# Sums of head outputs made in the out stage, x kept in its place (decoder layer, one core)

## The chip, the cores and the metric

The kernel runs on one core of one Trainium2 chip. A time is the device time of one execution in microseconds (us), and a version is judged by the median of its timed runs. Beside these, one execution was recorded by the hardware profiler. Its span is what the trace covers, and all moments named below count from the span's start. PE is the matmul engine (PEld its weight loads), DVE the vector engine, ACT the scalar engine, POOL the GpSimd engine; SP issues most DMAs, and its rows in the trace are issues, not transfers.

## The reference

One decoder layer on 256 rows of width 2048: attention in two groups of 8 heads, an output projection, and a feed-forward part. What matters here is the path from the head outputs over the projection to the input of the feed-forward part:

```python
h = rmsnorm(x, pre_mix_gain)
proj = jnp.einsum('bsd,de->bse', h, w_in)              # q, k, v of 16 heads, each 128 wide
o_sb = stick_breaking_attention(q_sb, k_sb, v_sb)      # heads 0 to 7
o_dl = dilated_attention(apply_rope(q_dl), apply_rope(k_dl), v_dl)   # heads 8 to 15
mixed = concatenate(head_rmsnorm(o_sb, gain), head_rmsnorm(o_dl, gain))   # 256 x 2048
mix_out = jnp.einsum('bse,ed->bsd', mixed, w_out)      # 2048 x 2048
x = x + rmsnorm(mix_out, post_mix_gain)
h = rmsnorm(x, pre_ffn_gain)
f = conv_geglu_ffn(h, w_up, conv_w, conv_b, w_down)    # w_up is 2048 x 11008
x = x + rmsnorm(f, post_ffn_gain)
```

Everything is float32.

## The kernel before

**Arithmetic.** A float32 product is made from rounded pieces: a weight tile `raw` is cast by ACT to `wh` (`high`, L161), DVE subtracts that from `raw` to give `wl` (`low`, L168), and the activations have such a pair as well. PE adds three matmuls for one product: high by high, low by high, high by low.

**Work and rings.** The weights come in chunks of 1 MB (1536 columns for some), listed in `chunks` in the order in which PE uses them. SP loads a chunk as two tiles of up to 128 x 1024 into a ring of five rooms (`raw`, `RAW_BUFS`); `ahead(i)` issues loads two chunks ahead and splits one chunk ahead. `wh` and `wl` have four rooms each. So a load waits until the tile five before it is split, and a cast waits until PE has read a tile some four before it. Beside this, DMAs from SP and POOL (`down.presum`, one step for most chunks) form sums of weight blocks in DRAM: `t13` and `t24` of the out projection (`t_out` in the profile) and of the last matrix (`t_kept`). The order on each engine is set by a scheduler from the order of the code; where `pin` is used, as in the seam between out projection and feed-forward part, the order of the code is kept.

**The attention stage** goes over the 16 heads with `v` and `qk` chunks. Each head is a generator that is advanced after chunks (`step`). The last lines of `stick_head` make the normalised output `y` of one of the heads 0 to 7, split it into `mix[0]` and `mix[1]`, and, after each odd head, form sums for the pair.

**The out stage** multiplies `mix` (rows are heads, 128 each) by `w_out` in four blocks of 512 columns, `c` = 0 to 3, and four blocks of 512 rows, `kq` = 0 to 3. Column blocks 0 and 1, and the lower half of the rows for column blocks 2 and 3 (heads 8 to 15), are plain: 24 matmuls for one `out(c, kq)`. For heads 0 to 7 and column blocks 2 and 3 the kernel uses seven block products in place of eight: a pair of heads (`m` = 0 to 3), two row tiles of `x` and two column blocks form a 2 x 2 by 2 x 2 block product, whose factors are single blocks (chunk `pa`) or sums of blocks (chunk `ts` or `pb`, loaded from `t_out`). The sums of head outputs that multiply them are in the tile `so`: four sums for each pair, in two pieces. The seven results gather in seven accumulators `o`, called `seven` in the code.

**Early sums.** The weight sums of the pairs m = 0 and 1 (`ts`) are loaded and split early, into two tiles `early`, which lie in the two rooms `hT0` and `hT1` of the transposed activations (free between attention and feed-forward part). Those of m = 2 and 3 (`pb`) go through the ordinary ring.

**x.** The tile `x1` holds x for the first norm. Its room is then given to `so`. At `out(3, 2)` a new `x1` is made in that room, and x is loaded a second time (L1122, two DMAs of 1 MB) for the residual.

**The seam.** For each row tile t, after its last out product: squares of `o` (`squares`, L628, ACT), their mean and the root (`mean`, `newton`, L638 to L653), `update` (L1156, DVE: x + r * mix_out), `turn` (L1164, PE transposes into `pth`), `highs` (L1170, ACT) and `lows` (L1176, DVE) that fill `hT` for the first products of the feed-forward part (`mmu`). In the pinned order ACT has three casts of feed-forward weights, and one square of x, between the end of tile 0 and the squares of tile 1:

```python
hs = [high(raw, "up") for raw in raws[i + 1]]
up0.append(low(raws[i + 1][0], hs[0], "up"))
hs.append(high(raws[i + 2][0], "up"))
square(0, 0)
```

The tile `mg` (2 x 2048 columns) takes the projected rows; its columns 1024 to 2047 are written only late in the out stage. The tile `sums` shares one room (tag `on`) with the normalised outputs of heads 8 to 15, which PE transposes.

Of the kernel before, what the change touches and what calls it, by code (L numbers as in the profile page):

```python
# [9 lines left out]
F32 = mybir.dt.float32  # L10
F32R = mybir.dt.float32r
# [5 lines left out]
P = 128  # L17
D = 2048
S = 256
# [16 lines left out]
NPAIR = 17  # L36
LATE_PAIRS = 2
HELD = 4
OUT_PAIRS, SPLIT_EARLY = 4, 2
SINGLE_BEHIND = (0, 2, 4, 5, 7, 9, 11, 12, 14)  # L40


# [59 lines left out]
def layer_kernel(ctx: ExitStack, tc: tile.TileContext, a, out: bass.AP):  # L102
    nc = tc.nc
    V, A, T, G = nc.vector, nc.scalar, nc.tensor, nc.gpsimd

    cpool = ctx.enter_context(tc.tile_pool(name="cpool", bufs=1))
# [14 lines left out]
    HALF = 1024  # L121
# [19 lines left out]
    early = []  # L141

    def split_early(raws, m):
        if not early:
            early.extend(cpool.tile([P, SPLIT_EARLY, 2, HALF], F32R, tag=f"hT{i}", name=f"early{i}") for i in range(2))
        both = []
        for raw, room in zip(raws, early):
            wh, wl = (room[:, m, i, :] for i in range(2))
            A.copy(wh, raw)
            V.tensor_tensor(wl, raw, wh.bitcast(F32), op=ALU.subtract)  # L150
            both.append((wh, wl))
        return both
# [109 lines left out]
    out_cols = lambda c, kq: chunks.append(("out", c, kq, a["w_o"][c, kq], 2048))  # L262
    out_sums = lambda kind, m: chunks.append((kind, m, 0, [k[m] for k in kept_out], 2048))
    out_raw = lambda m: chunks.append(("pa", m, 0, a["w_op"][:, 1536 * m:1536 * (m + 1)], 1536))
    out_cols(0, 0)
    out_cols(0, 1)
    out_sums("ts", 0)
    out_cols(0, 2)
    out_cols(1, 0)
    out_sums("ts", 1)  # L270
    for c, kq in ((1, 1), (1, 2), (0, 3), (1, 3)):
        out_cols(c, kq)
    for m in range(3):
        out_raw(m)
    out_cols(2, 2)
    out_sums("pb", 2)
    out_raw(3)
    out_sums("pb", 3)
# [5 lines left out]
    raws, parts_of, between = {}, {}, {}  # L284
# [24 lines left out]
    hT = [Halves(hT2.tiles, i) for i in range(2)]  # L309

    phA = tc.tile_pool(name="phA", bufs=2)
    apool = phA.__enter__()
    cst = apool.tile([P, C_END - P], F32, name="cst", bufs=1)
    gpre = small.tile([P, KT], F32, name="gpre", bufs=1, padded_shape=[P, KT + 32])
    x1 = apool.tile([P, 2, D], F32, tag="x1", name="x1", bufs=1)
    x1_kept = nc.dram_tensor("x1_kept", (S, D), F32, kind="Internal").ap()

    mix = [apool.tile([P, NH, S], F32R, name=f"mix{i}", bufs=1) for i in range(2)]
    mg = apool.tile([P, 2, D], F32, name="mg", bufs=1)
# [134 lines left out]


    vts = {}
    even, so = [None], []

    banks = []

# [22 lines left out]
    def stick_head(h, qk):  # L483
# [47 lines left out]
        q = apool.tile([P, S], F32, tag="sq", name="q", bufs=1)  # L531
# [2 lines left out]
        V.scalar_tensor_tensor(q, q, 3.0, r0, op0=ALU.subtract, op1=ALU.mult)  # L534
        if h == 0:
            V.tensor_scalar(gain[:, 0:NH], par[:, P_HEAD:P_HEAD + NH], -0.5, None, op0=ALU.mult)
        y = q if h % 2 else apool.tile([P, S], F32, tag="jks", name="even", bufs=1)
        V.scalar_tensor_tensor(y, po, gain[:, h:h + 1], q, op0=ALU.mult, op1=ALU.mult)
        A.copy(mix[0][:, h, :], y)
        V.tensor_tensor(mix[1][:, h, :], y, mix[0][:, h, :].bitcast(F32), op=ALU.subtract)  # L540
        if h % 2 == 0:
            even[0] = y
            return
        m = h // 2
        if m == 0:
            so.append(apool.tile([P, OUT_PAIRS, 2, 4, P], F32R, tag="x1", name="so", bufs=1))
        sums = apool.tile([P, 4, P], F32, tag="on", name="sums", bufs=1)
        a11, a21, a12, a22 = even[0][:, 0:P], even[0][:, P:S], y[:, 0:P], y[:, P:S]
        V.tensor_tensor(sums[:, 0, :], a11, a21, op=ALU.subtract)
        V.tensor_tensor(sums[:, 1, :], a22, a21, op=ALU.subtract)  # L550
        V.scalar_tensor_tensor(sums[:, 2, :], sums[:, 1, :], -1.0, a11, op0=ALU.mult, op1=ALU.subtract)
# [463 lines left out]
    for i, (kind, p, s, _, w) in enumerate(chunks):  # L1015
        parts = ahead(i, 0 if (kind, p, s) == ("out", 3, 3) else SPLITS)
        if kind == "v":
            if s == 0:
                pool, tag = (ps_at, "at") if p == 1 else (ps_mm, "mm")
# [35 lines left out]
        elif kind == "qk":  # L1055
# [7 lines left out]
            if s == 1:  # L1063
                active.append(stick_head(p, qk) if p < 8 else dilated_head(p, qk))
                next(active[-1])
# [46 lines left out]
        elif kind == "out":  # L1112
# [4 lines left out]
                    rows = Rows(mg, "o")  # L1117
            if p == 3 and s == 2:
                held = parts
                x1 = apool.tile([P, 2, D], F32, tag="x1", name="x1", bufs=1)  # L1120
                for t in range(2):
                    nc.sync.dma_start(x1[:, t, :], a["x"][t * P:(t + 1) * P, :])  # L1122
                continue
            if p < 3:
                mm_moving(mm["out", p], parts, mix[0], mix[1], 4 * s, s == 0, s == 3, **(dict(skip_group_check=True) if p == 2 else {}))
                if s == 3:
# [11 lines left out]
            else:  # L1138
# [41 lines left out]
                hT = [Halves(hT2.tiles, i) for i in range(2)]  # L1180
                loose = dict(skip_group_check=True)
                wh, wl = (w[:, 0:512] for w in held[0])
# [200 lines left out]
```

## Time and profile before

| | us |
|---|---|
| median of three timed runs | 1091.31 |
| the three runs | 1088.06 to 1104.67 |
| the profiled execution, device time | 1087.02 |
| its span | 1085.2 |
| PE busy | 1069.1 (99%) |
| DVE busy | 852.7 (79%) |
| ACT busy | 683.8 (63%) |
| POOL busy | 108.9 (10%) |

The profiled execution is 1.8 us longer than its span, and 4.3 us under the median of the timed runs. PE counts as busy from the start of a matmul to its modelled end, so a busy PE may still be waiting briefly between matmuls; idle time of the other engines costs nothing as long as PE has work. The attention stage ends at about 304 us, the out stage lasts to 386, the seam to about 400, and the feed-forward part takes the rest. Rows of the trace are read as: start, duration, engine, line, operation, written tile <- read tiles, count, and in square brackets how long the engine was idle before it and what ended that.

### The profile page before, as it was taken

The numbers are of one execution on the slowest core, as the hardware profiler recorded it, in microseconds if no ns is written. First come the engines' busy times: TensorE is split into PE (matmuls) and PEld (weight loads), VectorE is DVE, ScalarE is ACT, GpSimd is POOL, SyncE is SP. The second block draws the span as 40 slices with busy tenths as digits, with TensorE's granted clock in tenths as the row PEclk, the third lists the DMA queues.
The fourth block names the chain that finished last, engine by engine and source line by source line (L and its number), as shares of the span: only waits on it lengthen the run. The fifth ranks groups of instructions, "written<-read, shape, count | busy, mean of one in ns | idle before, by whom it ended". The sixth has DMA issues, their size and how long they took to land.

```text
span 1085.2 us, 19025 instructions
## 1 busy us (share of the span) xinstructions
PE 1069.1 (99%) x7157; PEld 977.0 (90%) x7157; DVE 852.7 (79%) x1303; ACT 683.8 (63%) x1004; POOL 108.9 (10%) x143
## 2 busy tenths in 40 slices
PE   9999999999999989999999999999999999999996
PEld 7888888888888879999999999999999988888885
DVE  7577876876875778887877878787778699998997
ACT  6667767756764576565655555555555587666775
POOL 0011001111111001121111111111110100000002
PEclk9999999999999999999999999999999999999999
DMA  9998778899898879999999988999999899779993
GB/s 347 360 296 262 211 233 254 235 272 256 243 327 253 279 260 288 333 324 314 330 299 284 276 269 272 275 269 281 276 285 264 266 349 382 269 262 353 394 361 118
DMA packets 101596, 311.52 MB, mean 287 GB/s; under 512 B 10944, under 2 KB 11712, under 8 KB 96320
## 3 DMA queue, kind: packets, MB, share of 16 engines
q1 hardware_dynamic: 94832, 275.68, 71.4%
q0 software_dynamic: 6240, 34.09, 17.7%
q8 instruction: 56, 0.92, 0.3%
q10 hardware_dynamic: 432, 0.53, 0.1%
q14 instruction: 36, 0.29, 0.1%
HBM read 306.07 MB, written 72.35 MB: 349 GB/s over the span
## 4 chain that ended last, share of the span: by engine, by line
PE 92%; DVE 3%; DMA 2%; ACT 2%; issue 1%; DVEq 0%; ACTq 0%
PE mmu L193 42%; PE mmqk L183 9%; PE p L878 6%; PE p L877 6%; PE p L876 6%; PE mmqk L181 5%; PE mmv L230 3%; PE mmv L231 3%; PE mmv L234 3%; DMA raw<-in_w_up 1%; PE mmo L234 1%; PE mmo L230 1%; PE mmo L231 1%; PE mmu L204 1%; DMA raw<-in_w_o 1%; DVE wl L168 1%
## 5 line engine op out<-in xcount | busy, mean ns | idle before, releaser
L168 DVE TENSOR_TENSOR wl<-raw,wh 128x1024 fp32r<-128x1024 f32 x383 | 454.5, 1194 | 161.2 <-ACT wh L161 129.9
L161 ACT CAST wh<-raw 128x1024 fp32r<-128x1024 f32 x383 | 391.8, 1029 | 178.2 <-PE mmu L193 62.9
L193 PE MATMUL mmu<-hT,wh 128*128 128x256 f32 x2688 | 311.9, 276 | 0.0
L193 PEld LDWEIGHTS mmu<-hT,wh 128*128 128x128 f32 x2688 | 308.1, 188 | 0.0
L193 PE MATMUL mmu<-hT,wl 128*128 128x256 f32 x1344 | 159.6, 276 | 0.0
L193 PEld LDWEIGHTS mmu<-hT,wl 128*128 128x128 f32 x1344 | 155.7, 188 | 0.0
L183 PE MATMUL mmqk<-hT,wh 128*128 128x512 f32 x512 | 122.0, 390 | 0.0
L183 PEld LDWEIGHTS mmqk<-hT,wh 128*128 128x128 f32 x512 | 94.8, 188 | 18.9
L692 ACT ACTIVATE cv<-pair,par 128x256 f32<-128x256 f32 x86 | 51.5, 599 | 80.9 <-DVE pair L690 80.5
L786 POOL DMA_DIRECT2D t_kept<-in_w x68 | 53.3, 885 | 351.4 <-DMA t_kept<-in_w_dn 340.3
L876 PE MATMUL p<-wh,yp 128*128 128x512 f32 x210 | 81.7, 389 | 0.0
L877 PE MATMUL p<-wh,yp 128*128 128x512 f32 x210 | 81.7, 389 | 0.0
L878 PE MATMUL p<-wl,yp 128*128 128x512 f32 x210 | 81.7, 390 | 0.0
L181 PE MATMUL mmqk<-hT,wl 128*128 128x256 f32 x512 | 67.9, 279 | 0.0
L181 PEld LDWEIGHTS mmqk<-hT,wl 128*128 128x128 f32 x512 | 63.5, 188 | 1.3
L786 POOL DMA_DIRECT2D t_kept<-t_kept x46 | 35.6, 774 | 266.3 <-DMA t_kept<-t_kept 135.2
L693 DVE SCALAR_TENSOR_TENSOR cv<-pair,par,cv 128x255 f32<-128x255 f32 x86 | 41.2, 480 | 14.8 <-ACT cv L692 14.8
L230 PE MATMUL mmv<-wh,hT 128*128 128x512 f32 x128 | 49.8, 391 | 0.0
L231 PE MATMUL mmv<-wh,hT 128*128 128x512 f32 x128 | 49.7, 390 | 0.0
L878 PEld LDWEIGHTS p<-wl,yp 128*128 128x128 f32 x210 | 39.4, 188 | 8.4 <-DVE wl L168 0.4
L877 PEld LDWEIGHTS p<-wh,yp 128*128 128x128 f32 x210 | 39.4, 188 | 8.3
L876 PEld LDWEIGHTS p<-wh,yp 128*128 128x128 f32 x210 | 39.4, 188 | 8.2
(301 smaller groups left out, 1349.7 us busy)
## 6 DMA issues: line engine op xcount, KB each, us to landing
raw<-in_w_up SPq DMA_DIRECT2D x172, 512.0 KB, 6.4
raw<-in_w_qk SPq DMA_DIRECT2D x64, 512.0 KB, 6.1
t_kept<-in_w_dn SPq DMA_DIRECT2D x57, 512.0 KB, 7.0
t_kept<-in_w POOLq DMA_DIRECT2D x68, 256.0 KB, 6.7
raw<-in_w_dn SPq DMA_DIRECT2D x31, 512.0 KB, 6.3
raw<-t_kept SPq DMA_DIRECT2D x29, 512.0 KB, 6.2
raw<-in_w_v SPq DMA_DIRECT2D x28, 512.0 KB, 5.6
raw<-in_w_o SPq DMA_DIRECT2D x24, 512.0 KB, 5.9
```

The source lines that it names most:

```text
L161: pin(A.copy(wh, raw))
L168: pin(V.tensor_tensor(wl, raw, wh.bitcast(F32), op=ALU.subtract))
L181: T.matmul(ps[:, 0, :], w, h[:, k, 0, :], **edge)
L183: T.matmul(ps, w, h[:, k, :, :], **edge)
L193: pin(T.matmul(ps, w, h[:, k, part, :], start=(i == 0), stop=(i == 3 * KT - 1)))
L230: T.matmul(ps[t], hi[:, k, tc_], ws, start=(first and i == 0 and j == 0), stop=False, **kw)
L231: T.matmul(ps[t], lo[:, k, tc_], ws, start=False, stop=False, **kw)
L692: A.activation(cv, u, AF.Identity, scale=cw(2), bias=par[:, P_CB + f:P_CB + f + 1])
L786: tc.keep_in_program_order(G.dma_start(flat(to), flat(block), accum_op=ALU.add, max_dma_last_dim=8192))
L876: T.matmul(ps, yh, wh[:, cs], start=key not in self.begun, stop=False)
L877: T.matmul(ps, yl, wh[:, cs], start=False, stop=False)
L878: T.matmul(ps, yh, wl[:, cs], start=False, stop=self.left[key] == 0)
```

## The change

1. The normalised output `y` of each of the heads 0 to 7 is written to `mg`, columns 1024 to 2047 (`whole(h)`), not to a passing tile. The sums of a pair are no longer made at the end of each odd head: the code moves to `head_sums(m)`, called in the out stage at the chunks `out(1,0)`, `out(1,1)`, `out(1,2)` and `out(0,3)`.
2. `so` lies in the room `hT0`, and `x1` keeps its room. The second load of x goes.
3. Since `hT0` is taken, only one pair (m = 0) is split early, into one tile in `hT1`. The weight sums of m = 1 become a `pb` chunk, and the chunks of the out stage stand in another order.

The diff, without the parts that only rename:

```diff
-OUT_PAIRS, SPLIT_EARLY = 4, 2
+OUT_PAIRS, SPLIT_EARLY = 4, 1
...
-            early.extend(cpool.tile([P, SPLIT_EARLY, 2, HALF], F32R, tag=f"hT{i}", name=f"early{i}") for i in range(2))
+            early.append(cpool.tile([P, 2, 2, HALF], F32R, tag="hT1", name="early"))
...
-        for raw, room in zip(raws, early):
-            wh, wl = (room[:, m, i, :] for i in range(2))
+        for n, raw in enumerate(raws):
+            wh, wl = (early[0][:, n, i, :] for i in range(2))
...
-    out_cols(0, 0)
-    out_cols(0, 1)
+    for c, kq in ((0, 0), (0, 1), (0, 2), (1, 0)):
+        out_cols(c, kq)
     out_sums("ts", 0)
-    out_cols(0, 2)
-    out_cols(1, 0)
-    out_sums("ts", 1)
     for c, kq in ((1, 1), (1, 2), (0, 3), (1, 3)):
         out_cols(c, kq)
-    for m in range(3):
-        out_raw(m)
+    out_raw(0)
+    out_raw(1)
+    out_sums("pb", 1)
     out_cols(2, 2)
+    out_raw(2)
     out_sums("pb", 2)
...
-        y = q if h % 2 else apool.tile([P, S], F32, tag="jks", name="even", bufs=1)
+        y = whole(h) if h < 2 * OUT_PAIRS else q
...
-        if h % 2 == 0:
-            even[0] = y
-            return
-        m = h // 2
+
+    def whole(h):
+        return mg[:, h // 4, 1024 + h % 4 * S:1024 + (h % 4 + 1) * S]
+
+    def head_sums(m):
         if m == 0:
-            so.append(apool.tile([P, OUT_PAIRS, 2, 4, P], F32R, tag="x1", name="so", bufs=1))
+            so.append(cpool.tile([P, OUT_PAIRS, 2, 4, P], F32R, tag="hT0", name="so"))
         sums = apool.tile([P, 4, P], F32, tag="on", name="sums", bufs=1)
-        a11, a21, a12, a22 = even[0][:, 0:P], even[0][:, P:S], y[:, 0:P], y[:, P:S]
+        a11, a21, a12, a22 = (whole(2 * m + k)[:, t * P:(t + 1) * P] for k in range(2) for t in range(2))
         V.tensor_tensor(sums[:, 0, :], a11, a21, op=ALU.subtract)
         V.tensor_tensor(sums[:, 1, :], a22, a21, op=ALU.subtract)
         V.scalar_tensor_tensor(sums[:, 2, :], sums[:, 1, :], -1.0, a11, op0=ALU.mult, op1=ALU.subtract)
...
             if p == 3 and s == 2:
                 held = parts
-                x1 = apool.tile([P, 2, D], F32, tag="x1", name="x1", bufs=1)
-                for t in range(2):
-                    nc.sync.dma_start(x1[:, t, :], a["x"][t * P:(t + 1) * P, :])
                 continue
+            if (p, s) in ((1, 0), (1, 1), (1, 2), (0, 3)):
+                head_sums(len(done))
+                done.append(p)
```

What this does to the order on the engines, at three places. First SP's queue from the last chunks of the out stage into the seam (`x_3899` is the second tile for x, `x_81` the first). Before:

```order
L129 DMA raw<-in_w_o 128x1024 x6
L782 DMA t_kept<-in_w_dn 128x2x512
L129 DMA raw<-in_w_up 128x1024 x2
L1122 DMA x_3899<-in_x 128x2048 x2
L129 DMA raw<-in_w_up 128x1024 x3
L1149 DMA x_kept<-x_3899 128x2048
L129 DMA raw<-in_w_up 128x1024
```

And now:

```order
L129 DMA raw<-in_w_o 128x1024 x6
L782 DMA t_kept<-in_w_dn 128x2x512
L129 DMA raw<-in_w_up 128x1024 x5
L1149 DMA x_kept<-x_81 128x2048
L129 DMA raw<-in_w_up 128x1024
```

The two loads of x between the second and the third load of feed-forward weights are gone; nothing else moved there.

Second, SP's queue where the seven products run (`in_w_op` is a `pa` chunk, `t_out` a chunk of weight sums). Before:

```order
L129 DMA raw<-in_w_op 128x1024
L129 DMA raw<-in_w_op 128x512
L129 DMA raw<-in_w_o 128x1024 x2
L137 DMA raw<-t_out 128x2x512 x2
L129 DMA raw<-in_w_op 128x1024
L129 DMA raw<-in_w_op 128x512
L137 DMA raw<-t_out 128x2x512 x2
```

And now:

```order
L137 DMA raw<-t_out 128x2x512 x2
L129 DMA raw<-in_w_o 128x1024 x2
L129 DMA raw<-in_w_op 128x1024
L129 DMA raw<-in_w_op 128x512
L137 DMA raw<-t_out 128x2x512 x2
L129 DMA raw<-in_w_op 128x1024
L129 DMA raw<-in_w_op 128x512
L137 DMA raw<-t_out 128x2x512 x2
```

Three loads of weight sums stand here where there were two, and the third `pa` chunk has gone behind `out(2,2)`.

Third, DVE in the out stage, at the last of the heads (`head_674`) and the splits of the following chunks. Before:

```order
L605 TENSOR_SCALAR on<-head_674,rr 128x128 x2
L168 TENSOR_TENSOR wl<-raw,wh 128x1024 x2
L613 SCALAR_TENSOR_TENSOR mix_83<-head_674,par,mix_82 128x256
L168 TENSOR_TENSOR wl<-raw,wh 128x1024 x5
L632 SCALAR_TENSOR_TENSOR mg<-mmo,gbc 128x512
```

And now:

```order
L605 TENSOR_SCALAR on<-head_674,rr 128x128 x2
L168 TENSOR_TENSOR wl<-raw,wh 128x1024
L549 TENSOR_TENSOR sums<-mg 128x128
L550 TENSOR_TENSOR sums<-mg 128x128
L168 TENSOR_TENSOR wl<-raw,wh 128x1024
L551 SCALAR_TENSOR_TENSOR sums<-sums,mg 128x128
L613 SCALAR_TENSOR_TENSOR mix_83<-head_674,par,mix_82 128x256
L552 TENSOR_TENSOR sums<-mg,sums 128x128
L168 TENSOR_TENSOR wl<-raw,wh 128x1024
L554 TENSOR_TENSOR so<-sums,so 128x512
```

The five instructions of a pair's sums stand between the splits of weight tiles, one pair for each chunk; the rows of the other three pairs follow in the same way.

More of the change, by code (lines that the diff above doesn't have):

```diff
@@ L314, in layer_kernel @@
     gpre = small.tile([P, KT], F32, name="gpre", bufs=1, padded_shape=[P, KT + 32])
-    x1 = apool.tile([P, 2, D], F32, tag="x1", name="x1", bufs=1)
+    x1 = apool.tile([P, 2, D], F32, name="x1", bufs=1)
     x1_kept = nc.dram_tensor("x1_kept", (S, D), F32, kind="Internal").ap()
@@ L456, in layer_kernel @@
     vts = {}
-    even, so = [None], []
+    so, done = [], []
     banks = []
@@ L1119, in layer_kernel @@
                 held = parts
-                x1 = apool.tile([P, 2, D], F32, tag="x1", name="x1", bufs=1)
-                for t in range(2):
-                    nc.sync.dma_start(x1[:, t, :], a["x"][t * P:(t + 1) * P, :])
                 continue
+            if (p, s) in ((1, 0), (1, 1), (1, 2), (0, 3)):
+                head_sums(len(done))
+                done.append(p)
             if p < 3:
```

## The prediction

> **What bounds the kernel now.** I read the busy times by stage first, then what PE waited for, then the chain of waits where the two meet. The stages, with PE, PEld, DVE, ACT and POOL busy, the granted clock, the DMA share and GB/s:
> ```profile
> 300.00:344.00 44.00, 43.85 (x210) 35.96 (x209) 29.67 (x55) 25.05 (x53) 6.31 (x8) 1.00 0.95 298
> 344.00:369.00 25.00, 25.00 (x112) 20.68 (x111) 15.41 (x16) 14.04 (x17) 0.00 (x0) 1.00 0.75 236
> 369.00:386.00 17.00, 17.00 (x82) 14.23 (x81) 15.28 (x24) 7.41 (x13) 1.56 (x2) 1.00 0.99 353
> 386.00:400.00 14.00, 8.88 (x62) 7.94 (x60) 10.44 (x24) 10.28 (x27) 0.00 (x0) 0.88 0.72 274
> 400.00:700.00 300.00, 300.00 (x2644) 299.92 (x2644) 237.71 (x376) 173.01 (x228) 44.40 (x57) 1.00 0.94 295
> 700.00:1060.00 360.00, 360.00 (x2316) 326.17 (x2315) 306.24 (x389) 232.94 (x274) 19.35 (x25) 1.00 0.92 306
> ```
> PE has work without a break in the out stage (300 to 386) and again from 400 to 1060. What is won or lost before 400 therefore moves everything behind it by the same amount. Only the seam, 386 to 400, has PE idle (5.1 of 14 us), and there the clock is below full. The waits of PE:
> ```profile
> PE pth L1164 <- DVE x L1156: 4.9, 1, 4.9
> ...
> PE score L567 <- DVE qk L562: 0.7, 2, 0.4
> ```
> The long one is the transposes of the second row tile, which wait for the residual `x`. The chain of waits there (start, us, what):
> ```profile
> 372.20 14.88 DMA raw<-in_w_up
> ...
> 388.86 0.70 ACT jks L628 x2
> ...
> 390.70 0.50 DVE x L1156
> ...
> 391.25 0.70 PE pth L1164 x2
> ```
> So the cause is a weight load that took 14.9 us. The timeline of SP, ACT, DVE and PE shows how it reaches PE:
> ```profile
> 370.85 0.99 SPq L1122 DMA_DIRECT2D x<-in_x  x2
> 372.20 0.33 SPq L129 DMA_DIRECT2D raw<-in_w_up  x1
> ...
> 381.63 1.98 ACT L161 CAST wh<-raw 128x1024 fp32r<-128x1024 f32 x2
> 387.16 1.04 ACT L161 CAST wh<-raw 128x1024 fp32r<-128x1024 f32 x1 [3.54 <-DMA raw<-in_w_up]
> ...
> 384.87 1.22 DVE L168 TENSOR_TENSOR wl<-raw,wh 128x1024 fp32r<-128x1024 f32 x1
> 389.58 0.16 DVE L638 TENSOR_SCALAR_CACHE_REDUCE rj<-sso 128x4 f32<-128x4 f32 x1 [3.49 <-ACT jks L628]
> ...
> 384.42 0.62 PE L234 MATMUL o<-wl,mix 128*128 128x512 f32 x2
> 384.87 1.47 PE L1164 MATMUL pth<-ident,x 128*128 128x128 f32 x12
> 391.25 1.12 PE L1164 MATMUL pth<-ident,x 128*128 128x128 f32 x4 [4.90 <-DVE x L1156]
> ```
> SP issues two loads of `x` just ahead of that weight load. ACT then reaches the cast of the weight early and stands 3.54 us in it. The squares of the second row tile (`jks`) are queued behind the cast, the norm (`rj`) behind the squares, the update of `x` behind the norm, PE behind the update.
>
> **The change, part by part.**
>
> *The two loads of x go.* How long loads take from issue to landing (KB each, us), around the seam:
> ```profile
> raw<-in_w_up SPq DMA_DIRECT2D x1, 512.0 KB, 7.6
> ...
> x<-in_x SPq DMA_DIRECT2D x2, 1024.0 KB, 12.9
> ```
> The one weight load issued just before x took 7.6 us, so the late one would land at 372.2 + 7.6 = 379.8. By the other way, 2.1 MB fewer at the stage's 353 GB/s are 5.9 us, and 387.1 - 5.9 = 381.2. ACT wants it at 381.63 + 1.98 = 383.6, so on either count the wait is gone with 2.4 us or more to spare. What is late next: everything on ACT moves 3.55 us up, and the squares of the second tile, at 388.86 before, would start at 385.31. Their input is ready when PE ends its last `o` product, 384.42 + 0.62 = 385.04, so PE's own work is only 0.27 us from being the limit. DVE would reach `rj` at 389.58 - 3.55 = 386.03, but is busy until 384.87 + 1.22 = 386.09. So 0.06 us is lost and the term is **-3.5 us**; PE's gap shrinks from 4.9 to 1.4 us. Bounds: 0, if the load is as late without x, and -3.5.
>
> *The clock.* The page's row of granted clock over 40 slices, the slices around PE's restart, and ACT's waits for transposes there:
> ```profile
> PEclk9999999999999999999999999999999999999999
> ...
> 390.00:391.00 1.00, 0.00 (x0) 0.00 (x0) 0.93 (x4) 0.81 (x3) 0.00 (x0) 1.00 0.94 389
> 391.00:392.00 1.00, 0.76 (x4) 0.61 (x4) 1.00 (x3) 0.03 (x1) 0.00 (x0) 0.57 0.38 156
> ...
> 393.97 1.57 ACT L1170 ACTIVATE hT<-pth,par 128x256 fp32r<-128x256 f32 x4 [0.43 <-PE pth L1164]
> ...
> 397.90 0.84 ACT L1170 ACTIVATE hT<-pth,par 128x256 fp32r<-128x256 f32 x2 [0.68 <-PE pth L1164]
> ```
> The seam's mean of 0.88 over 14 us is 14 x 0.12 / 0.5 = 3.4 us at half clock, beginning with PE's restart. Had PE alone set the pace, that cost 1.7 us. But ACT feeds PE there, and ACT itself waited for PE's slow transposes only 0.43 + 0.68 = 1.1 us. A gap of 4.9 us brought the clock down, gaps of 0.4 us (the `score` row, in the attention stage) did not, since every slice of the page reads 9 there. A gap of 1.4 us lies nearer to the second, so I take the clock to hold and the term to be **-1.1 us**, with bounds 0 and -1.7. [...]
>
> *The sums of head outputs move from the attention stage to the out stage.* One pair of heads costs (min/median/max ns):
> ```profile
> L549 DVE TENSOR_TENSOR sums<-even x4: 281/281/282, 117.4 to 218.9; 128x128 f32<-128x128 f32 x4
> ...
> L552 DVE TENSOR_TENSOR sums<-q,sums x4: 292/292/295, 119.9 to 221.2; 128x128 f32<-128x128 f32 x4
> L554 DVE TENSOR_TENSOR so<-sums,so x4: 686/692/693, 120.9 to 223.3; 128x512 fp32r<-128x512 f32 x4
> ...
> L553 ACT CAST so<-sums x4: 605/620/624, 120.2 to 222.0; 128x512 fp32r<-128x512 f32 x4
> ```
> That is 4 x 0.29 + 0.69 = 1.85 us of DVE and 0.62 us of ACT, four times: 7.4 and 2.5 us. Where they leave, PE waited for DVE only 0.7 us in all, so they give 0 (bounds 0 and -0.7). Where they arrive (in the stretch from 300 to 344), DVE was busy 29.7 of 44 us and has 37 after, and ACT 27.5. The cover is the ring of split weights: a tile is split three tiles before PE reads it, 3 x 2.7 us. Without that cover each sum would cost its 1.85 us. The first sum waits on DVE for PE's transposes of the last head (its room was theirs); the split of the next tile is queued behind it, with the same cover. **0 us.** Storing the heads' outputs in `mg` instead of `even` is the same instruction to another place: 0.
>
> *One pair's weight sums are no longer split early.* PE's count of products stays; the order of loads changes, and that has a cost only if loads come late. The pace of PE; then the loads in us from issue to landing (the first two rows for 340 to 369, the next row and the spread of the `t_out` loads for 284 to 312); then the split's two halves:
> ```profile
> 344.46 0.23 PE o L1084
> ...
> 355.34 0.23 PE o L1084
> ...
> raw<-in_w_o SPq DMA_DIRECT2D x8, 512.0 KB, 5.6
> raw<-t_out SPq DMA_DIRECT2D x4, 512.0 KB, 4.1
> ...
> raw<-t_out SPq DMA_DIRECT2D x4, 512.0 KB, 6.2
> ...
> DMA to landing us min/median/max: 4.6/6.2/7.0
> ...
> L168 DVE TENSOR_TENSOR wl<-raw,wh 128x1024 fp32r<-128x1024 f32 x10 | 12.1, 1224 | 6.7 <-ACT wh L161 6.6
> L161 ACT CAST wh<-raw 128x1024 fp32r<-128x1024 f32 x11 | 11.4, 1054 | 6.7 <-PE o L1084 4.4 <-PE o L231 1.2 <-DVE wl L168 0.7
> ```
> Sixteen products take 355.34 - 344.46 = 10.88 us, 0.68 each; the first starts at 344.2. In the new order `pa0` with the early sums ends at 349.0, `pa1` and `pb1` at 353.8, `out(2,2)` (8 x 0.68) at 359.2, `pa2` at 361.2, and `pb2`, `pa3`, `pb3` at 368.7 as before. A load goes out when the tile five before it is split. `pb1`'s second tile gets the room of `pa0`'s first (349.0) and is split by 349.0 + 1.05 + 1.22 = 351.3. Then `pb2`'s first tile is loaded, for a time L, and split at 353.6 + L; `pb3`'s second, five tiles on, at 355.9 + 2L. PE wants it at 368.7 - 1.36 = 367.3, so L may be 5.7 us. The weight sums took 4.1 us in this stretch, and the one pair added (1 MB) meets a DMA share of 0.75 there: I take L = 4.1 and **0 us**. At the longest `t_out` load of the out stage, 7.0 us, PE would lose 2 x (7.0 - 5.7) = 2.6 us. Bounds 0 and +2.6.
>
> **The sum.** -3.5 - 1.1 + 0 + 0 = -4.6 us. The profiled execution took 1087.0 us (span 1085.2 and 1.8 around it), so 1082.4 in its terms. The three timed runs have their median at 1091.3, 4.3 above it; against that median the forecast is 1086.7.
>
> **The rivals.**
> - *The clock falls all the same*: the 1.4 us gap is enough, and only -3.5 is left, 1087.8. For it: the seam after the gap is full of short waits for ACT. Against: the 0.4 us gaps.
> - *The load is late without x*: the DMA share was 0.99 from 369 to 386, and if other queues fill the room, the cast waits on. The gain is then 0 to 2 us, 1089 to 1091.3. Against: 7.6 us for the neighbour.
> - *The out stage runs dry, slower than before*: the place is `pb2` to `pb3`, the price 2 x (L - 5.7), and it decides when this exceeds 4.6, at L = 8.0. At L = 9 the time is 1091.3 - 4.6 + 6.6 = 1093.3. For it: 7.0 has been seen at the stage's start, with a higher DMA share. Against: 4.1 in the very stretch, and the two x loads that would compete later are gone.
>
> **How the numbers follow.** Forecast 0.65, clock falls 0.12, load late 0.10, out stage dry 0.08, anything else 0.05. The low end takes all best bounds, -3.5 - 1.7 - 0.7 = -5.9, from the profiled execution: 1081. The high end is the dry out stage: 1093. That leaves out less than 2 in 10. Two per cent, 22 us, is about what a measurement of this kernel can tell from no change, and no case comes near it: faster 0.01, same 0.97, slower 0.02.
>
> **What would show it.** Right: no wait of ACT's cast for `in_w_up` at the seam, PE's longest wait near 1.4 us, clock 1.00 throughout, and a start of the dense stretch some 4.6 us earlier. Wrong: the cast still waits for DMA; PE waits for `wh` or `wl` in 344 to 369; landings of `t_out` above 5.7 us. A new wait of PE anywhere before 344 would break the claim that the moved sums are covered.

## The result and the profile after

The changed kernel took 1082.57 us (median of 6 runs) against 1091.31 in the three runs shown ahead; run beside each other, the ratio of after to before is 0.9933, 95% interval 0.9908 to 0.9959. That is faster by 0.4 to 0.9%, inside the 2% that counts as no change, and 4 us below the forecast of 1086.7, though inside its range of 1081 to 1093. The first ratio rests on only two executions of the kernel before, 1088.06 and 1091.31. Two later sets of runs of the same two kernels gave 0.9960 (0.9944 to 0.9976) and 0.9952 (0.9932 to 0.9972). Some executions of a kernel are 17 us longer, with 281 ns for a product of the up stage instead of 276; the ratios, and the counts and medians below, leave them out, but the profiles of the changed kernel and of E1, E4, E6, E8, E10 and E11 are of such executions, so they are read only up to 410 us, and their last stretch is 0.41 us too long.

Four starts on PE divide the way there: the first product of the value projection at 148 us and of the next one at 222, the first of the seven products, the first transpose `pth`, and `r2ps` in the dense stretch. The timeline of PE in the kernel before (start, us, what):

```profile
148.45 0.39 PE L230 MATMUL mmv<-wh,hT 128*128 128x512 f32 x1
...
222.69 0.39 PE L230 MATMUL mmv<-wh,hT 128*128 128x512 f32 x1
...
344.07 0.39 PE L1083 MATMUL o<-wh,mix 128*128 128x512 f32 x1
...
401.32 1.07 PE L204 MATMUL mmu<-hT,wl 128*128 128x256 f32 x8
...
411.52 0.60 PE L660 MATMUL r2ps<-pair,negones 128*128 128x128 f32 x4
```

And in the changed kernel, with the two groups of transposes:

```profile
148.49 0.39 PE L230 MATMUL mmv<-wh,hT 128*128 128x512 f32 x1
...
221.48 0.39 PE L230 MATMUL mmv<-wh,hT 128*128 128x512 f32 x1
...
342.93 0.39 PE L1083 MATMUL o<-wh,mix 128*128 128x512 f32 x1
...
385.12 1.47 PE L1164 MATMUL pth<-ident,x 128*128 128x128 f32 x12
387.88 0.83 PE L1164 MATMUL pth<-ident,x 128*128 128x128 f32 x4 [1.29 <-DVE x L1156]
...
396.69 1.11 PE L204 MATMUL mmu<-hT,wl 128*128 128x256 f32 x8
...
407.30 0.61 PE L660 MATMUL r2ps<-pair,negones 128*128 128x128 f32 x4
```

With the `pth` rows of before, 384.87 and 391.25, the stretches between these starts are:

| stretch on PE (us) | before | changed | difference |
|---|---|---|---|
| 148 to 222, attention | 74.24 | 72.99 | -1.25 |
| 222 to the seven products | 121.38 | 121.45 | +0.07 |
| seven products to first `pth` | 40.80 | 42.19 | +1.39 |
| first `pth` to second | 6.38 | 2.76 | -3.62 |
| second `pth` to `r2ps` | 20.27 | 19.42 | -0.85 |
| sum | | | -4.26 |

The last stretch of the changed kernel can't be taken as it stands. From the row of eight products (L204) to `r2ps` the same products take 411.52 - 401.32 = 10.20 us before and 407.30 - 396.69 = 10.61 in the changed kernel. At the pace of before, the last difference is -1.26 and the sum -4.67. E12, whose profile has the pace of before, confirms it: second `pth` at 386.48, `r2ps` at 405.50, which is 19.02 us and 1.25 under before.

The seam did what was forecast, two other stretches moved by more than an us each, and these two nearly cancel. The stages of the changed kernel, with the columns of before (PE, PEld, DVE, ACT, POOL, clock, DMA share, GB/s):

```profile
300.00:344.00 44.00, 43.39 (x208) 35.97 (x207) 33.83 (x72) 27.54 (x58) 6.31 (x8) 1.00 0.90 270
344.00:369.00 25.00, 25.00 (x112) 20.67 (x111) 15.42 (x16) 14.07 (x15) 0.00 (x0) 1.00 0.79 265
369.00:386.00 17.00, 16.24 (x75) 12.88 (x74) 16.38 (x25) 10.70 (x19) 1.56 (x2) 1.00 0.86 273
386.00:400.00 14.00, 12.46 (x103) 11.59 (x102) 13.88 (x32) 12.04 (x33) 0.00 (x0) 1.00 0.76 264
```

The clock of the seam is 1.00 where it was 0.88, and PE is busy there 12.46 us where it was 8.88. But PE now has idle time in the two stages that had almost none. The waits of PE from 60 to 400 us (us in total, times, longest):

```profile
PE pth L1164 <- DVE x L1156: 1.3, 1, 1.3
PE head L609 <- DVE on L605: 0.6, 1, 0.6
PE o L230 <- DVE o L1110: 0.6, 1, 0.6
PE o L234 <- DVE wl L168: 0.2, 1, 0.2
PE mmu L204 <- ACT hT L1170: 0.2, 1, 0.2
```

The 4.9 us are 1.3, the two waits for scores (`L567`, 0.7) are gone, and three waits of the out stage and a short one in the seam are new.

*The seam.* ACT and DVE there (timeline):

```profile
381.85 2.93 ACT L161 CAST wh<-raw 128x1024 fp32r<-128x1024 f32 x3
...
385.43 0.60 ACT L628 ACTIVATE jks<-o 128x512 bf16<-128x512 f32 x1
...
386.22 0.15 DVE L638 TENSOR_SCALAR_CACHE_REDUCE rj<-sso 128x4 f32<-128x4 f32 x1
```

Three casts run through with no wait between them; before, the third stood 3.54 us. `rj` comes at 386.22, when DVE ends a split that began at 385.09, as the working had it.

*The loss of 1.39 us.* SP and ACT in the kernel before, from the loads of out(2,3) on:

```profile
358.40 9.46 SPq L129 DMA_DIRECT2D raw<-in_w_o  x6
...
366.39 1.06 ACT L161 CAST wh<-raw 128x1024 fp32r<-128x1024 f32 x1
```

SP, ACT and PE in the changed kernel:

```profile
359.98 6.74 SPq L129 DMA_DIRECT2D raw<-in_w_o  x6
...
359.22 1.57 ACT L161 CAST wh<-raw 128x1024 fp32r<-128x1024 f32 x2 [0.53 <-PE o L1084]
...
367.83 1.05 ACT L161 CAST wh<-raw 128x1024 fp32r<-128x1024 f32 x1 [2.72 <-DMA raw<-in_w_o]
...
374.27 0.50 PE L230 MATMUL o<-wh,mix 128*128 128x512 f32 x1 [0.58 <-DVE o L1110]
```

The casts at 366.39 and 367.83 are of the second tile of out(2,3), counted by the order and the widths of the casts. The first of the six `w_o` loads goes out at 359.98, 1.6 us later than the 358.40 of before, while PE was 1.1 us ahead. The second goes out at 361.56 (360.43 before), behind the split of the cast at 359.22, and takes 6.2 us; ACT waits 2.72 us for it. DVE's row sums (L1108 to L1132) stand behind that tile's split, and PE waits for them. By its starts PE loses 0.74 us at 374.27, where the view shows 0.58, and most of the other 0.65 around the wait for `wl` that the view shows as 0.2.

*The gain of 1.25 us.* It falls at two places, 203 and 216 us. ACT, DVE and PE of the kernel before at the first:

```profile
197.28 2.00 ACT L161 CAST wh<-raw 128x1024 fp32r<-128x1024 f32 x2
199.31 0.62 ACT L558 COPY rot<-qk 64x512 f32<-64x512 f32 x1
...
202.94 0.68 DVE L562 TENSOR_TENSOR qk<-qk,rot 128x512 f32<-128x512 f32 x1
...
202.54 0.84 PE L181 MATMUL mmqk<-hT,wl 128*128 128x256 f32 x5
203.68 0.49 PE L567 MATMUL score<-qk 128*128 128x128 f32 x2 [0.30 <-DVE qk L562]
```

And of the changed kernel:

```profile
196.53 1.05 ACT L161 CAST wh<-raw 128x1024 fp32r<-128x1024 f32 x1
197.60 0.62 ACT L558 COPY rot<-qk 64x512 f32<-64x512 f32 x1
...
200.22 0.69 DVE L562 TENSOR_TENSOR qk<-qk,rot 128x512 f32<-128x512 f32 x1
...
202.66 0.39 PE L567 MATMUL score<-qk 128*128 128x128 f32 x2
202.80 0.36 PE L480 MATMUL score<-qh 128*128 128x256 f32 x1
```

Before, the rotation copies stand on ACT behind two casts from 197.28 on, in the changed kernel behind one; on DVE a split of 1.2 us stands ahead of the last step of the rotation (L562) before, and behind it in the changed kernel. So the copies came 1.7 us later and the next head's finished rows 2.7, and PE had to wait for them behind five products of other work. In the changed kernel PE doesn't wait. No sum runs on DVE between 196 and 204 us in either trace; what differs in this stretch is the order of ACT's and DVE's queues. But in the kernel before a pair's sums end on DVE only at 195.83, and ACT begins the cast ahead of these rows at 195.78, in the changed kernel at 194.54. At the second place the copies come 2.1 us later before (212.36 against 210.27), and no sum runs there from 196 to 218.

### The profile page after: what moved, and what is told of

Read it like the earlier page. It is cut to its first block, busy times and chain, and to the rows that moved or that the text cites. A ratio compares the mean times of both kernels' runs of the same rounds, so it can differ in the third digit from the quotient of the medians.

```text
span 1098.0 us, 19018 instructions
## 1 busy us (share of the span) xinstructions
PE 1085.4 (99%) x7157; PEld 993.3 (90%) x7157; DVE 853.5 (78%) x1303; ACT 684.5 (62%) x1004; POOL 108.9 (10%) x143
## 4 chain that ended last, share of the span: by engine, by line
PE 95%; DVE 2%; DMA 1%; ACT 1%; issue 1%; DVEq 0%; ACTq 0%
PE mmu L193 43%; PE mmqk L183 11%; PE p L876 6%; PE p L878 6%; PE p L877 6%; PE mmqk L181 5%; PE mmv L230 3%; PE mmv L231 3%; PE mmv L234 3%; PE mmo L231 1%; PE mmo L234 1%; PE mmo L230 1%; PE mmu L204 1%; DVE wl L168 1%; DMA raw<-in_w_o 1%
## 5 line engine op out<-in xcount | busy, mean ns | idle before, releaser
L168 DVE TENSOR_TENSOR wl<-raw,wh 128x1024 fp32r<-128x1024 f32 (+1 forms) x385 | 456.7, 1194 | 176.4 <-ACT wh L161 139.9
L161 ACT CAST wh<-raw 128x1024 fp32r<-128x1024 f32 (+1 forms) x385 | 393.7, 1028 | 189.6 <-PE mmu L193 83.3
L193 PE MATMUL mmu<-hT,wh 128*128 128x256 f32 x2688 | 323.7, 281 | 0.0
L193 PEld LDWEIGHTS mmu<-hT,wh 128*128 128x128 f32 x2688 | 319.6, 189 | 0.0
L193 PE MATMUL mmu<-hT,wl 128*128 128x256 f32 x1344 | 165.5, 281 | 0.0
L193 PEld LDWEIGHTS mmu<-hT,wl 128*128 128x128 f32 x1344 | 161.6, 189 | 0.0
```

The lines of the kernel that those rows point to most:

```text
L161: pin(A.copy(wh, raw))
L168: pin(V.tensor_tensor(wl, raw, wh.bitcast(F32), op=ALU.subtract))
L193: pin(T.matmul(ps, w, h[:, k, part, :], start=(i == 0), stop=(i == 3 * KT - 1)))
```

## The experiments

Each kernel was run with a profile and in five rounds beside the kernel before. The stretches by the same starts, in us, and the ratio to before; the starts from which they are subtracted are PE's rows as above:

| kernel | 148 to 222 | to the seven | to `pth` | to `r2ps` | ratio (95%) |
|---|---|---|---|---|---|
| before | 74.24 | 121.38 | 40.80 | 26.65 | 1 |
| changed | 72.99 | 121.45 | 42.19 | 22.18 | 0.9933 (0.9908 to 0.9959) |
| E1 changed, again | 72.99 | 122.30 | 42.64 | 22.20 | 0.9960 (0.9944 to 0.9976) |
| E8 changed, third time | 72.99 | 121.33 | 42.16 | 22.24 | 0.9952 (0.9932 to 0.9972) |
| E2 sums moved only | 72.99 | 121.24 | 40.81 | 27.28 | 0.9989 (0.9978 to 0.9999) |
| E3 changed, x loaded | 73.00 | 121.40 | 42.18 | 27.13 | 1.0000 (0.9992 to 1.0009) |
| E4 before, cast later | 74.29 | 121.76 | 40.80 | 24.79 | 0.9956 (0.9942 to 0.9969) |
| E5 changed, pa2 ahead | 73.00 | 121.36 | 40.80 | 23.40 | 0.9939 (0.9920 to 0.9959) |
| E6 changed, early sums back | 73.00 | 120.87 | 42.41 | 22.16 | 0.9936 (0.9916 to 0.9955) |
| E7 both, seam edited | 73.00 | 120.87 | 40.81 | 22.54 | 0.9938 (0.9920 to 0.9956) |
| E11 the same, again | 72.99 | 120.87 | 41.90 | 22.91 | 0.9931 (0.9906 to 0.9956) |
| E12 both, seam as changed | 72.99 | 120.87 | 40.81 | 21.81 | 0.9938 (0.9925 to 0.9952) |
| E9 before, gap filled | 74.27 | 121.70 | 40.80 | 26.37 | 0.9986 (0.9977 to 0.9996) |
| E10 E7 with gap filled | 73.00 | 120.87 | 41.90 | 22.92 | 0.9940 (0.9920 to 0.9960) |

In the last stretch the changed kernel, E1, E4, E6, E8, E10 and E11 hold the 0.41 us named above. The first stretch repeats far better than the times do: 148 to 222 is 74.24 to 74.29 in three kernels whose attention is as before, and 72.99 or 73.00 in eleven with the sums moved.

**E1, the changed kernel again.**

> The changed kernel once more, to get the size of the change from more executions. My reading of its trace against the trace before, by moments of the same instruction: the first out product of the seven comes 1.2 us earlier (342.9 for 344.1), the first transposes of the seam 0.25 later, the second ones 3.4 earlier, the first feed-forward products after the seam (r2ps) 4.2 earlier. So I expect 4.2 to 4.6 us under the kernel before, a ratio of 0.996. The rival: the 0.9933 of the first measurement (7.3 us) is the true size, and some 3 us come from a place that one pair of traces doesn't show.

The ratio is the 0.9960 expected, and 0.9933 lies outside its interval: the rival found no support. In the profile the wait at head 14 (L609) is 1.4 us instead of 0.6, and the one for L1110 is 1.0 instead of 0.6: these waits vary.

**E2, only the sums moved.** The kernel before with the sums made in the out stage; they stay in the room of `x1`, so x is loaded again, two pairs are split early and the loads keep their order:

```
-        y = q if h % 2 else apool.tile([P, S], F32, tag="jks", name="even", bufs=1)
+        y = whole(h) if h < 2 * OUT_PAIRS else q
...
+            if (p, s) in ((1, 0), (1, 1), (1, 2), (0, 3)):
+                head_sums(len(done))
+                done.append(p)
```

> The kernel before with one part of the change: the outputs of heads 0 to 7 kept in mg and the sums of pairs made in the out stage; so stays in the room of x, x is loaded a second time, two pairs of weight sums are split early, and the chunks stand in the old order. Theory: the 1.2 us won before the seven products come from DVE and ACT work taken out of the attention stage; then the first of the seven products stands near 342.9 here too, the gap of PE at the seam stays 4.9 us with the clock falling, and the kernel is about 1 us faster than before (ratio 0.999). Rival: they come from the new order of loads; then the first product stays at 344.1 and the ratio is 1.000.

PE and ACT of this kernel:

```profile
221.41 0.39 PE L230 MATMUL mmv<-wh,hT 128*128 128x512 f32 x1
```

```profile
196.47 1.05 ACT L161 CAST wh<-raw 128x1024 fp32r<-128x1024 f32 x1
197.54 0.62 ACT L559 COPY rot<-qk 64x512 f32<-64x512 f32 x1
```

The attention stage gives the whole 1.25 us, with ACT in the order of the changed kernel, and the out stage loses nothing (121.24 and 40.81). So the gain in attention belongs to the moved sums, and the loss in the out stage does not. Whether it comes from DVE's time for the sums or from the order that the scheduler chose without them isn't separated. The time fell only 0.1%: the seam took 27.28, 0.6 more than before, with the clock at half for 6.8 us instead of 3.4.

**E3, the changed kernel with x loaded after all.** Two loads of 1 MB at the old place, into a room that nothing reads:

```
+                again = cpool.tile([P, 2, D], F32, tag="hT0", name="again")
+                for t in range(2):
+                    nc.sync.dma_start(again[:, t, :], a["x"][t * P:(t + 1) * P, :])
```

> The changed kernel with the two 1 MB loads of x put back at their old place in SP's queue, into the room hT0, which is empty then; nothing reads them. Theory: the loads alone make the third feed-forward weight load late (about 15 us for 5.8), ACT waits 3 to 4 us in the cast, PE's gap is again near 4.9 us and the clock falls to half for 3.4 us; the kernel loses 4 to 4.5 us and comes out level with the kernel before (ratio 0.999 to 1.002). Rival: the loads are hidden and the gain came from elsewhere; then the ratio stays at 0.996.

ACT of this kernel in the seam:

```profile
386.61 1.04 ACT L161 CAST wh<-raw 128x1024 fp32r<-128x1024 f32 x1 [2.98 <-DMA raw<-in_w_up]
```

The late weight, the gap (4.3 us) and the fall of the clock (mean 0.994, as in E2) are back, and the whole gain is gone: ratio 1.0000. This settles the seam. It also shows that the 1.38 us lost ahead of `pth` have nothing to do with the x loads, which go out behind the late ones.

**E4, the kernel before with the third cast behind the squares of row tile 1.** x is still loaded:

```
-                        hs.append(high(raws[i + 2][0], "up"))
                         square(0, 0)
+                hs.append(high(raws[i + 2][0], "up"))
                 square(0, 1)
```

> The kernel before with one line moved: the third cast of feed-forward weights stands behind the squares, mean and root of the second row tile on ACT, not ahead of them. The two loads of x stay and the weight load stays late. Theory: what cost the time was what is queued behind the cast, not the late load itself; PE's gap falls to 1.3 to 1.6 us, the clock holds at 1.00, and the kernel is 4 us faster than before (ratio 0.996). Rival: the late load stops something else at once (the cast is needed by the next feed-forward products); then the gap moves from the transposes to the products and the gain is under 1 us.

PE's gap here, and two slices behind it:

```profile
388.61 0.83 PE L1164 MATMUL pth<-ident,x 128*128 128x128 f32 x4 [2.10 <-DVE x L1156]
```

```profile
389.00:390.00 1.00, 0.46 (x4) 0.22 (x3) 1.00 (x2) 1.00 (x4) 0.00 (x0) 0.77 1.12 385
390.00:391.00 1.00, 1.00 (x5) 1.00 (x5) 1.00 (x3) 1.00 (x3) 0.00 (x0) 0.50 0.82 332
```

By the times, one line moved gives as much as the whole change does (0.9956). The profile shows only 1.9 us less from the first `pth` to `r2ps`, or 2.3 without the 0.41; the clock fell in it, behind a gap of 2.1 us, and the rest of the gain is not shown there. The gap stays at 2.1 us because the update of row tile 0 waits 0.81 us for x itself, and DVE's split follows it.

**E5, the third `pa` chunk put back ahead of out(2,2).**

```
-    out_cols(2, 2)
     out_raw(2)
+    out_cols(2, 2)
```

> The changed kernel with the third pa chunk put back ahead of out(2,2), where it stood before the change; nothing else differs. Theory (the changed kernel loses about 1.4 us in the last part of the out stage because pb2's second tile must wait for the room of out(2,2)'s second tile, freed at 357.6, so that the loads of out(2,3) to out(3,3) go out about 1.6 us too late): with pa2 ahead the room is freed some 2 us earlier, ACT's wait of 2.72 us for the first tile of out(2,3) falls under 1.5 us, DVE's row work (o, L1110) comes earlier, PE's waits for it (0.6) and for wl (0.2) go, the first transpose pth starts at about 384.0 instead of 385.1 and the time falls by 0.8 to 1.4 us, ratio to before about 0.994 to 0.995 where the changed kernel stands at 0.996. Rival (those loads take 6.2 to 6.8 us because six of them and the neighbours share the DMA queues; when they start hardly matters): they stay at 6 to 7 us, the waits stay, first pth within 0.3 us of 385.1, no change of time.

SP, ACT and PE of this kernel:

```profile
358.34 8.54 SPq L129 DMA_DIRECT2D raw<-in_w_o  x6
```

```profile
366.81 1.06 ACT L161 CAST wh<-raw 128x1024 fp32r<-128x1024 f32 x1 [0.35 <-DMA raw<-in_w_o]
```

```profile
383.90 1.47 PE L1164 MATMUL pth<-ident,x 128*128 128x128 f32 x12
386.69 0.83 PE L1164 MATMUL pth<-ident,x 128*128 128x128 f32 x4 [1.32 <-DVE x L1156]
```

The loads go out 1.6 us earlier, ACT's wait of 2.72 us for the second tile of out(2,3) is gone (the 0.35 shown is for the tile behind it; the expectation took the 2.72 for the first tile's), both of PE's waits are gone, and the stretch is back at 40.80. So the order of chunks made the loss here. It isn't the only way to it: E10 and E11, with the same order, have 41.90. There ACT waits 2.73 and 2.32 us for the second tile of `pb2` (`t_out`), where E5 and E12 have 1.00 and 1.12; the `w_o` loads go out at 359.3 and 359.4 instead of 358.2 to 358.3, and the second tile of out(2,3) is late again by 2.4 us. Why those loads took longer is open. The median time is about 1 us under the changed kernel's, but the intervals overlap. The clock fell in this profile. Its slices:

```profile
388.00:389.00 1.00, 1.00 (x8) 1.00 (x6) 1.00 (x3) 0.93 (x4) 0.00 (x0) 0.57 0.96 373
389.00:390.00 1.00, 1.00 (x6) 1.00 (x6) 1.00 (x2) 1.00 (x4) 0.00 (x0) 0.50 0.38 156
390.00:391.00 1.00, 1.00 (x7) 1.00 (x6) 1.00 (x4) 1.00 (x3) 0.00 (x0) 0.50 0.95 401
391.00:392.00 1.00, 1.00 (x8) 1.00 (x8) 1.00 (x3) 1.00 (x3) 0.00 (x0) 0.72 1.02 393
```

Half clock for 3.4 us, behind a gap as short as that of the changed kernel, where it held. Against E12, which has the same seam and kept its clock, the fall cost 23.40 - 21.81 = 1.6 us.

**E6, the early weight sums at their old place.**

```
-    for c, kq in ((0, 0), (0, 1), (0, 2), (1, 0)):
-        out_cols(c, kq)
+    out_cols(0, 0)
+    out_cols(0, 1)
     out_sums("ts", 0)
+    out_cols(0, 2)
+    out_cols(1, 0)
```

> The changed kernel with the one early pair of weight sums loaded and split at its old place, behind out(0,1) instead of behind out(1,0). Theory (the wait of PE for head 14's norm, 0.6 to 1.4 us at L609, comes from the early splits, which now stand ahead of that norm on ACT and DVE and wait for their load there): the wait is gone, the first o product of the seven starts at about 342.3 instead of 342.9, everything behind it 0.6 us earlier, time 0.6 us less. Rival (the norm is late for the sums of heads that DVE now makes in this stage, 1.85 us a pair): the wait stays at 0.6 or more, first o product within 0.2 us of 342.9, time the same.

The wait at head 14 is gone and the seven products start 0.6 us earlier. In the profile the tail of the out stage gives 0.2 of it back (42.41, PE's wait for L1110 is 0.8 instead of 0.6). The intervals of E6 and of the changed kernel overlap, so a difference in time isn't shown.

**E7 and E11, both orders and an edited seam.** The fourth update of row tile 0 and the first squares go behind the norm of row tile 1:

```
-                        for c in range(4):
+                        for c in range(3):
                             update(0, c)
...
-                        square(0, 0)
-                square(0, 1)
+                square(0, 0, 1)
...
                 update(1, 1)
+                update(0, 3)
```

> The changed kernel with both edits (third pa chunk ahead of out(2,2), early sums at their old place) and a third one in the seam: the fourth update of row tile 0 and the squares of its first columns stand behind the norm of row tile 1 instead of ahead of it. Theory: the first two bring 1.4 to 2.0 us together; in the seam rj moves from 1.1 us behind PE's last o product (386.22 against 385.1) to about 0.6 us behind it, PE's gap of 1.3 us falls to 0.8 us, the clock stays at 1.00; in all 1.9 to 2.5 us under the changed kernel, about 1080 us, ratio to before 0.992 to 0.994. Rival: the update moved behind delays the transposes of the later columns by its 0.69 us, the gap returns in pieces there, and only the first two edits count, 1.4 to 2.0 us; or they overlap and give under 1 us.

The two orders brought their 0.6 and 1.4 us. The seam edit failed: the gap fell to 1.1 us, not 0.8, PE's waits for `hT` on ACT rose from 0.2 to 0.7 us, and the stretch is 22.54 where E12 has 21.81. E11 is the same kernel:

> The kernel of e7 once more, beside the one with a filled gap. By its first runs: 1080.6 to 1081.4 us where nothing disturbs it, ratio to before 0.992 to 0.996; first pth 383.2, gap 1.1 us, r2ps 405.7.

Its ratio repeats, and so does its seam, 22.91 less the 0.41; its profile shows late tiles again (41.90), with PE waiting 0.3 and 0.2 us for L1112 and `wl`.

**E8, the changed kernel a third time**, as the yardstick.

> The changed kernel once more, beside the three versions above, as their yardstick. By the runs so far: ratio to before 0.995 to 0.997, 1082 us where the clock holds in the seam; span 1080 to 1081 in the profile, first o product of the seven at 342.9, first pth at 385.1, PE's gap 1.3 us. If the clock falls in the seam in some executions although the gap is 1.3 us, these take 1 to 4 us longer and show a mean clock of 0.996 or 0.995 instead of 0.997 to 0.998.

Of its thirteen executions in three sets, ten took 1081.6 to 1082.6 us but for one of 1084.4, at a mean clock of 0.997 or 0.998; three had 0.995 or 0.996 and took 1083.5, 1083.8 and 1085.8.

**E9 and E10, the gap filled.** Extra products on PE, overwritten by the last transposes (19 in E9, 4 in E10):

```
+                        pts[5] = ps_mm.tile([P, 2, S], F32, tag="mm", name="pth")
+                        for n in range(19):
+                            pin(T.matmul(pts[5].rearrange("p a b -> p (a b)"), mix[0][:, 8, 0:P],
+                                         mix[0][:, 8:10, :].rearrange("p a b -> p (a b)"), start=True, stop=True))
+                        turn(0, 5)
```

> The kernel before with 19 extra products of 512 columns put on PE between the transposes of row tile 0 and those of row tile 1, into a bank that the last transposes overwrite; they fill PE's gap of 4.9 us with 19 x 0.23 = 4.3 us of work whose result nothing reads. [...] Rival (the clock's fall hides behind ACT, and what the changed kernel won behind the gap came from its earlier work on ACT and DVE): the clock holds but r2ps stays at 411.2 to 411.6 and the time is the same within 0.3 us.

The seam of E9, and a wait that is new in it:

```profile
386.00:400.00 14.00, 12.21 (x83) 10.30 (x81) 10.62 (x23) 10.88 (x29) 0.00 (x0) 1.00 0.77 293
```

```profile
396.32 0.85 PE L1164 MATMUL pth<-ident,x 128*128 128x128 f32 x6 [1.20 <-DVE hT L1176]
```

The clock held in the profile and in all nine executions compared (0.997 or 0.998), and the time fell by 0.04 to 0.23%, although the second transposes came only 0.2 us earlier, 6.20 us behind the first instead of 6.38. The profile itself shows only 0.3 us less in the seam, since the order of PE's work behind the gap shifted and a wait of 1.2 us came with it. So the clock has a price of its own, and its size here rests on the times.

> The kernel with both orders and the shorter seam (e7), with four such extra products (0.9 us) in its gap of 1.1 us. [...] Rival (the clock falls by something else than PE's gap): executions with 0.995 or 0.996 are as frequent as in the changed kernel, 1 in 4.

E10 had three executions that are compared, all at 0.997 or 0.998, at 1080.9, 1082.7 and 1082.9 us: too few to tell how often the clock falls with the gap filled.

**E12, the two orders alone.**

> The changed kernel with the two changes of order alone (third pa chunk ahead of out(2,2), early sums at their old place), the seam as the changed kernel has it. Theory (each of the two orders takes away its own wait, and the third edit of e7 cost 0.35 us): from the first mmv product at 148 us to the first of the seven products 193.9 us (changed kernel 194.4), from there to the first pth 40.8 (changed kernel 42.2), from there to r2ps 22.2 where the clock holds (e7 22.5); together 1.9 us under the changed kernel, 1080.3 to 1080.7 us, ratio to before 0.992 to 0.994. Rival (the two overlap: the early sums give nothing once the later loads come in time): the sum of the three stretches falls by 1.4 us only, as in e5.

PE's waits from 284 to 400 us:

```profile
PE pth L1166 <- DVE x L1158: 1.3, 1, 1.3
PE mmu L204 <- ACT hT L1172: 0.2, 1, 0.2
```

In this profile nothing is left but the gap of the seam and 0.2 us behind it. Each order removes its own wait, and they add: 120.87 and 40.81, together 2.0 us under the changed kernel up to `pth`; `r2ps` is at 405.50. The times, 1080.7 to 1082.8, lie about 1 us under the changed kernel's; E5, E6, E7 and E12 can't be ranked by their times. This is the version to keep, by its trace: faster than before by 0.5 to 0.75%, and simpler than E7. Its orders don't take away the loss ahead of `pth` in every execution, as the 41.90 of E10 and E11 shows.

## Why the prediction was right and wrong

**The x loads: right.** Forecast -3.5 us and a gap of 1.4; measured -3.62 and 1.3, with no wait in the cast. E3 brings the whole loss back by the loads alone. E4 shows the other half of the cause: with the loads in place, moving the cast that waits for them frees most of the path as well.

**The clock: right in size, its reason only in part.** Forecast -1.1; the stretch behind the second `pth` is 0.85 us shorter as measured, 1.26 at one pace of the products. In E2, where the clock is at half for 6.8 us, and in E3 the mean clock is 0.994. Over 48 executions of the kernel before, the 22 with a mean clock of 0.994 have their median at 1088.5 us and the 12 with 0.997 at 1087.4, so such a fall, part of which lies in PE's gap (in E2 the slice from 387 to 388 has 0.91, and PE resumes at 389.71), goes with about 1 us there. But the working chose by the length of the gap, and that doesn't decide: a gap of 1.3 us kept the clock in the changed kernel's profile and lost it in E5's. So the rival that the clock falls all the same came true in some executions, by their mean clock in three of the thirteen above. Nor could the page's row of nines show that gaps of 0.4 us are harmless, since its slice with the seam reads 9 as well; slices of 5 us do show it, with 1.00 from 0 to 1075 in the trace of before but from 390 to 395. Half clock lasted 3.4 us in before, E4 and E5, behind gaps of PE of 4.9, 2.1 and 1.3 us, and 6.8 us in E2, where the gap was 4.8; what sets it off no run shows.

**The moved sums in attention: the step that failed, and in which direction.** "PE waited for DVE only 0.7 us in all, so they give 0 (bounds 0 and -0.7)." They gave 1.25 us, beyond the bound. The 0.7 us quoted were the very two waits that went (L567 for L562), but the view undercounts them. At 202.54 five products are shown as busy for 0.84 us, though fifteen of the same kind just ahead take 1.87 us; the modelled end of the last one reaches beyond its turn, and the wait is counted from there as 0.30. By starts alone PE lost more: the first rows of the next head, 214.72 and 214.18, stand 66.27 and 65.69 us behind the 148 mark, which is 0.58 at the first place and leaves 0.67 of the 1.25 for the second. And 0 was taken where the row named a gain. E2 shows that the moved sums bring it; whether by DVE's time or by the order of the queues stays open.

**The moved sums in the out stage: right.** DVE is busy 33.8 us of 44 where it was 29.7, and E2 shows no loss. The new wait at head 14 is not theirs: E6 removes it by moving the early splits, which the working had at nothing.

**The order of loads: the second failed step.** "I take L = 4.1 and 0 us." L was right: the four `t_out` loads from 344 to 369 took 4.0 us (median). The bound of +2.6 holds the +1.39, but the place was wrong: the working followed the ring up to `pb3`, and it broke one chunk later, at out(2,3). It let `pb2` be split as soon as it had landed, at 353.6 + L, and so left out the four rooms of `wh` and `wl`. With the third `pa` chunk now between out(2,2) and `pb2`, the second tile of `pb2` gets the room of out(2,2)'s second tile instead of that of the `pa` chunk; PE is done with it later, and the load that follows this split is the first of out(2,3). Likewise the first tile of `pa3` gets the room of the moved chunk's first tile, and behind its split goes the load for which ACT waits 2.72 us. The rival of a dry out stage was the right kind, at another place and mostly by another wait: PE waits 0.2 us for a split weight, and 0.6 for row sums queued on DVE behind a late tile.

**The two errors nearly cancel**, -1.25 against +1.39. By this luck the forecast sum of -4.6 meets the -4.67 of the two traces, while two of its four terms were wrong.

**The 4.3 us put on for the median: the failed step that moved the number.** "The three timed runs have their median at 1091.3, 4.3 above it; against that median the forecast is 1086.7." 1091.3 was one high execution: of 48 later ones of the same kernel 46 lie between 1086.0 and 1089.7, their median at 1088.0, 1.0 above the profiled one. 1087.0 - 4.6 = 1082.4, which the working had in hand, is what the changed kernel took. These 4.3 us account for all of the 4.1 us by which the forecast of 1086.7 misses 1082.57.

## What to carry to other kernels

Where work is removed from an engine that feeds the bound, follow the few rows of waits to their places and take their length from the starts of the instructions, since a modelled end hides part of each wait. Where chunks change places in a ring of buffers, follow every chunk up to the end of the stage: count the rooms of every ring that a tile passes, and look one chunk beyond the ones that moved. Here the late load was there, and the wait came up on PE by way of another engine's queue. A median of three runs is no offset; forecast from the profiled execution when it lies among the quick ones.

## What the runs showed of the hardware

The half clock lasted 3.4 us in before, E4 and E5 and 6.8 us in E2, and in E5 it began 1.4 us after PE had resumed work, following a gap of 1.3 us. Behind the same gap of 1.3 us the clock stayed at 1.00 in the profiles of the changed kernel, E8 and E12 (slices of 1 us, 386 to 400); E1 and E6, with that gap too, have the changed kernel's mean clock, 0.998. So behind a gap this short it fell in one profile of six. Part of the scatter between executions of one kernel, about 1 us, goes with the clock of this one place: in the profile of before it is the only slice of 5 us, from 0 to 1075, under 1.00 (0.66 from 390 to 395), and in E8 to E12 no slice of 1 us from 0 to 1073 is.
